# Strassen's seven products for the up projections of a streaming encoder layer

## The chip, the cores and the metric

One NeuronCore of one Trainium2 chip runs the whole layer in one launch. The metric is the device time of that launch in microseconds. Engine names below: PE is TensorE (matmul), PEld its weight loads, DVE is VectorE, ACT is ScalarE, POOL is GpSimd, SP is the engine that issues all DMAs here.

## The reference

One layer over 2048 new frames and 32 frames of a running stream (2080 tokens, model width 1024, hidden width 2816). The mixer (stick-breaking attention beside a state-space model) comes first, then the part that this change is about:

```python
def conv_ffn(h, conv_prev, p):
    gu = h @ p['w_up']                                   # (tokens, 1024) x (1024, 2 * 2816)
    gate, up = gu[..., :D_FF], gu[..., D_FF:]
    gate_c, conv_new = causal_dwconv(gate, conv_prev, p['ffn_conv_w'], p['ffn_conv_b'])   # width 3
    act = jax.nn.gelu(gate_c, approximate=True) * up
    return act @ p['w_down'], conv_new

x = x + rmsnorm(m, p['g_mix_post'])                      # m: output of the mixer
f, ffn_conv_new = conv_ffn(rmsnorm(x, p['g_ffn_pre']), ffn_conv_prev, p)
x = x + rmsnorm(f, p['g_ffn_post'])
```

All of it is float32.

## The kernel before

**Precision.** A float32 product is made of three matmuls in the fast format fp32r: each operand is split into a rounded part (hi) and the rest (lo), and `dense` issues hi x hi, hi x lo and lo x hi for each chunk of 128 of the contracted width. A weight is split once: `weight` loads the raw tile, ACT rounds it (L110), POOL subtracts (L111), and the pair is also stored to a scratch tensor in DRAM (`wS_...`). Whoever asks for the same weight later recalls hi and lo with one DMA (L106), twice the raw bytes. Three weight buffers of 128 x 2 x 8 x 128 rotate in the pool `weights`, and two raw ones.

**Blocks.** Tokens lie along the free dimension and are cut into four blocks, `SBS`: three of 512 and the last of 544, which holds the 32 frames of the running stream and is worked on as two tiles of 272 (`tiles_of`). A first phase makes the input projection and the state-space part of all blocks. Then the attention of block s+1 (`Attention.heads`) runs with the tail of block s (`Tail.stream`) as filler: a generator that yields after a few matmuls, from which `heads` takes a given number of steps per attention slot (`count` gives the sum of steps). `pin` and `mark` keep PE's filler matmuls behind the attention matmul that they follow in the program; attention is not held behind filler in that way. The tail of block 3 has no attention beside it (`alone`).

**A tail.** `stream` takes, in this order: 8 steps of what the block before still owes; the output projection of half the tokens (`out_units`, 256 wide, or 272 in block 3), then of the other half, with the residual of the first half (`residual`: normalize, add x, store to DRAM, square and sum) taken a step at a time in between; `root` and `residual` of the second half; `split`, which makes hi and lo of the unnormalized tokens times the gain (L981, L982); and the rest of what is owed, namely the down projections of the last two groups of the block before. The root of the mean square (`root`, `rstd_narrow`) isn't needed by `split`: it multiplies gate when that leaves PSUM (L1015), and up's factor cancels only in the norm after the down projection, which is told so by `rcol`. Then come the 22 hidden tiles j in groups of three (the last groups of two, or one of four in block 3). `up` makes gate j (bank `o`, 24 matmuls per token tile), the convolution over the tokens, the GeLU, up j (bank `u`), the product, and its hi and lo. After the first j of a group stands the `down` projection of the group before. `finish` normalizes and writes the block before, a step here and there.

The order of instructions on each engine is made at build time from a simulated timeline with priorities by program order. PE, DVE, ACT and POOL then work off their own lists in order, and SP issues DMAs in order, so a DMA that waits for its buffer holds up those behind it.

Of the kernel before, what the change touches and what calls it, by code (L numbers as in the profile page):

```python
# [18 lines left out]
STORE = True  # L19
WBUFS = 3  # L20
RBUFS = 2
# [39 lines left out]
class Kernel:  # L61
# [35 lines left out]
    def weight(self, pool, src, n=KC, key=None, tag=None):  # L97

        nc = self.nc
        w = pool.tile([P, 2, KC, P], F32R, name=tag or "w", bufs=1 if tag else self.wbufs)  # L100
        hi, lo = w[:, 0], w[:, 1]
        keys = key if isinstance(key, list) else [key]
        if keys[0] in self.kept:
            m = n // len(keys)
            for i, k in enumerate(keys):
                nc.sync.dma_start(w[:, :, m * i : m * i + m, :].bitcast(F32), self.kept[k][:])  # L106
            return hi, lo
        raw = self.wp.tile([P, KC, P], F32, name="wraw", bufs=RBUFS)
        nc.sync.dma_start(raw[:, :n, :], src)
        nc.scalar.copy(hi[:, :n, :], raw[:, :n, :])  # L110
        nc.gpsimd.tensor_tensor(lo[:, :n, :], raw[:, :n, :], hi[:, :n, :].bitcast(F32), op=ALU.subtract)  # L111
        if key is not None and STORE:
            d = self.kept[key] = self.dp.tile([P, 2, n, P], F32, name="wS_" + "_".join(map(str, key)))
            nc.sync.dma_start(d[:], w[:, :, :n, :].bitcast(F32))
        return hi, lo
# [4 lines left out]
    def dense(self, ps, w, x, c0, c1, ks=KC, k0=0, first=True, last=True, pin=False):  # L120
        nc = self.nc
        (whi, wlo), (xhi, xlo) = w, x
        at = lambda t, k: t[k] if isinstance(t, list) else t[:, k, :]
        for k in range(ks):
            for i, (l, r) in enumerate(((whi, xhi), (whi, xlo), (wlo, xhi))):
                mm = nc.tensor.matmul(  # L126
                    ps[:, : c1 - c0],
                    l[:, k, :],
                    at(r, k0 + k)[:, c0:c1],
                    start=first and i == 0 and k == 0,  # L130
                    stop=last and i == 2 and k == ks - 1,
                )
# [434 lines left out]
def gate(kn, s, xs, xc, r0, tm):  # L567
# [3 lines left out]
    for c in range(4):  # L571
        w = kn.weight(kn.wp, kn.a["wz"][c])
        for c0, c1 in tiles:
            n = c1 - c0
            ps = kn.po.tile([P, 512], F32, name="o")
            for k in range(KC):
                kn.dense(ps, [t[:, k : k + 1, :] for t in w], xs, c0, c1, ks=1, k0=k, first=k == 0, last=k == KC - 1, pin=s == NSB - 1)
                if len(tiles) == 1 or k % 2:
                    yield
# [317 lines left out]
class Tail:  # L897
# [7 lines left out]
    def __init__(self, kn, att, ctx, pu):  # L905
# [13 lines left out]
        self.owed = None  # L919

    def out_units(self, s, cat, half):
# [3 lines left out]
        if c0 == 0:  # L925
            self.m = [self.mp.tile([P, 544], F32, name=f"m{c}") for c in range(KC)]
            self.msq = att.tmp.tile([P, 544], F32, name="msq")
            self.w = {}
        back = list(range(KC - WBUFS, KC))
        for i, c in enumerate(range(KC) if c0 == 0 else back + list(range(KC - WBUFS))):  # L930
# [8 lines left out]
            for k in (4, 5, 6, 7, 0, 1, 2, 3):  # L939
                kn.dense(ps, [t[:, k : k + 1, :] for t in w], cat, c0, c1, ks=1, k0=k, first=k == 4, last=k == 3, pin=self.pin)  # L940
# [54 lines left out]

    def up(self, s, j, acts):
# [5 lines left out]
        wg = kn.weight(kn.wp, kn.a["wup"][j], key=("up", j))  # L1002
# [4 lines left out]
        for c0, c1 in tiles_of(nt):  # L1007
            ps = self.po[0].tile([P, 512], F32, name=self.po[1])
            for k in range(KC):
                kn.dense(ps, [t[:, k : k + 1, :] for t in wg], self.x, c0, c1, ks=1, k0=k, first=k == 0, last=k == KC - 1, pin=self.pin)  # L1010
# [26 lines left out]
        wu = kn.weight(kn.wp, kn.a["wup"][NJ + j], key=("up", NJ + j))  # L1037
        for c0, c1 in tiles_of(nt):
            ps = self.pu[0].tile([P, 512], F32, name=self.pu[1])
            for k in range(KC):  # L1040
                kn.dense(ps, [t_[:, k : k + 1, :] for t_ in wu], self.x, c0, c1, ks=1, k0=k, first=k == 0, last=k == KC - 1, pin=self.pin)
# [13 lines left out]
    def down(self, s, g, acts, tiles, end=False):  # L1055
# [10 lines left out]
        for c in range(0, KC, 2):  # L1066
            hi, lo = kn.weight(
                kn.wp, kn.a["wdn"][c // 2][:, 2 * j0 : 2 * j0 + 2 * n, :], 2 * n, key=[("dn", 6, c), ("dn", 7, c)] if n == 4 else ("dn", g, c)
            )
            for e in range(2):  # L1070
                w = hi[:, e : 2 * n : 2, :], lo[:, e : 2 * n : 2, :]
                for c0, c1 in tiles:
                    ps = self.po[0].tile([P, 512], F32, name=self.po[1])
                    for k in range(n):
                        kn.dense(ps, [t[:, k : k + 1, :] for t in w], acts, c0, c1, ks=1, k0=k, first=k == 0, last=k == n - 1, pin=self.pin)
                        if k < n - 1:
                            yield
                    dst = f[c + e][:, c0:c1]
                    if g == 0:
                        nc.scalar.copy(dst, ps[:, : c1 - c0])  # L1080
                    else:
                        nc.vector.tensor_tensor(dst, ps[:, : c1 - c0], dst, op=ALU.add)  # L1082
                    if end and s == NSB - 1 and c + e == KC - 1:
                        self.fsq1 = att.tmp.tile([P, 272], F32, name="sqt", bufs=2)
                        nc.scalar.activation(self.fsq1[:, : c1 - c0], f[KC - 1][:, c0:c1], AF.Square)
                    elif end:
# [237 lines left out]
```

## Time and profile before

| what | value |
|---|---|
| median of 3 runs | 2943.15 us (2933.8 to 2943.42) |
| span of the profiled execution | 2945.7 us, mean granted clock 0.978 |
| PE busy | 2816.0 us, 96% of the span |
| PEld, DVE, ACT, POOL busy | 82%, 58%, 42%, 43% |
| moved by DMA | 586.36 MB, 199 GB/s over the span |

The execution's own time is its span, from the first to the last instruction of the program; nothing around it is recorded here, and it stands 2.5 us above the median. By the order of time, up projections begin about 885 us (block 0), 1391 us (block 1), 1957 us (block 2) and 2512 us (block 3) after the start. In the lists below, a group's line reads: line of the kernel, engine, operation, output<-inputs, shapes, count, then busy us, mean ns of one, idle us before it and who ended it. A line of a window reads: busy us (instructions) of PE, PEld, DVE, ACT, POOL, the granted clock, the mean busy share of the DMA engines, GB/s. A line of the transfers reads: output<-input, queue, count, KB each, median us from issue to landing.

### The profile page before, as it was taken

How to read it: one execution, taken by the hardware profiler on the slowest of the kernel's cores; microseconds unless marked ns; L12 is line 12 of the kernel's file. 1: busy time of each engine (PE TensorE's matmuls, PEld its weight loads, DVE VectorE, ACT ScalarE, POOL GpSimd, SP SyncE). 2: the span in 40 equal slices, each digit the busy share in tenths (PEclk: the TensorE clock that was granted, in tenths of full speed). 3: DMA queues.
4: the chain of work that ended last, by engine and by line, in shares of the span. 5: the costliest groups of instructions: out<-in, count | busy, mean ns of one | idle time of the engine just before them, and what ended most of it. 6: DMA issues, size and time to landing. Idle time of an engine off the chain costs nothing.

```text
span 2945.7 us, 44837 instructions
## 1 busy us (share of the span) xinstructions
PE 2816.0 (96%) x16699; PEld 2427.4 (82%) x16699; DVE 1696.8 (58%) x2628; ACT 1250.6 (42%) x2534; POOL 1273.1 (43%) x1083
## 2 busy tenths in 40 slices
PE   8999999989889999999999999999999999999997
PEld 6777787977778888888788888978888889899997
DVE  7667576557774555537644455786666652623333
ACT  4344444337665444436433334664444443311111
POOL 4565555435676656547422222553223234511113
PEclk9999999989999999999999999999999999999998
DMA  5646463648677777777555556656554445755555
GB/s 179 183 143 187 145 173 120 173 131 271 223 266 246 267 266 251 271 261 249 194 190 182 179 171 212 247 175 219 179 175 165 167 160 200 242 183 172 170 183 194
DMA packets 251308, 586.36 MB, mean 199 GB/s; under 512 B 66154, under 2 KB 107762, under 8 KB 222546
## 3 DMA queue, kind: packets, MB, share of 16 engines
q1 hardware_dynamic: 251090, 583.49, 59.9%
q8 instruction: 133, 2.18, 0.3%
q14 instruction: 85, 0.70, 0.1%
HBM read 445.70 MB, written 137.69 MB: 198 GB/s over the span
## 4 chain that ended last, share of the span: by engine, by line
PE 74%; DVE 12%; DMA 7%; ACT 2%; issue 2%; POOL 1%; SPq 1%; DVEq 0%; POOLq 0%; ACTq 0%
PE o L126 36%; PE u L126 12%; PE t L126 11%; PE z L821 4%; PE pa L862 4%; PE pt L840 3%; PE o L370 2%; DVE xc L346 2%; DMA acB<-acD 1%; DVE prow L672 1%; DMA w<-wS_out 1%; DVE acB L446 1%; DVE xc L342 1%; DVE x L268 1%; DMA xr<-hS 1%
## 5 line engine op out<-in xcount | busy, mean ns | idle before, releaser
L126 PE MATMUL o<-xhi,w 128*128 128x512 f32 (+2 forms) x3968 | 1047.4, 346 | 30.1 <-ACT xhi L292 7.7
L126 PEld LDWEIGHTS o<-xhi,w 128*128 128x128 f32 x3968 | 698.2, 192 | 124.2 <-ACT xhi L292 7.7
L126 PE MATMUL o<-xlo,w 128*128 128x512 f32 (+2 forms) x1984 | 683.8, 345 | 6.9 <-DVE xlo L278 4.2
L111 POOL TENSOR_TENSOR w<-wraw,w 128x1024 fp32r<-128x1024 f32 (+2 forms) x156 | 369.0, 2366 | 228.2 <-ACT w L110 207.1
L677 POOL TENSOR_TENSOR beta<-beta,prow 128x512 f32<-128x512 f32 (+3 forms) x256 | 255.0, 998 | 429.1 <-DVE prow L672 345.5
L126 PEld LDWEIGHTS o<-xlo,w 128*128 128x128 f32 x1984 | 380.5, 192 | 51.7 <-DVE xlo L278 6.1
L1036 POOL TENSOR_TENSOR y<-y,gb 128x512 f32<-128x512 f32 (+1 forms) x88 | 115.8, 1317 | 544.4 <-ACT gb L1035 544.4
L126 PE MATMUL u<-xhi,w 128*128 128x512 f32 x1056 | 349.4, 398 | 0.0
L126 PE MATMUL o<-ah,w 128*128 128x512 f32 x992 | 342.5, 403 | 3.1 <-DVE f L1082 3.0
L845 DVE TENSOR_TENSOR wt<-pt,wt 128x512 fp32r<-128x512 f32 (+2 forms) x320 | 191.7, 602 | 156.5 <-ACT wt L844 153.9
L672 DVE TENSOR_TENSOR_SCAN prow<-gam,prow,z 128x513 f32<-128x513 f32 x192 | 245.3, 1277 | 61.5 <-ACT beta L670 58.9
L844 ACT CAST wt<-pt 128x512 fp32r<-128x512 f32 (+2 forms) x320 | 167.5, 526 | 208.7 <-PE pt L840 207.1
L126 PEld LDWEIGHTS u<-xhi,w 128*128 128x128 f32 x1056 | 199.1, 189 | 46.6
L126 PEld LDWEIGHTS o<-ah,w 128*128 128x128 f32 x992 | 187.5, 189 | 45.4 <-DVE f L1082 3.9
L669 ACT ACTIVATE gam<-z 128x512 f32<-128x512 f32 (+2 forms) x320 | 173.3, 542 | 95.5 <-PE z L821 69.8
L126 PE MATMUL u<-xlo,w 128*128 128x512 f32 x528 | 209.4, 397 | 0.0
L110 ACT CAST w<-wraw 128x1024 fp32r<-128x1024 f32 (+2 forms) x156 | 155.2, 995 | 124.7 <-PE o L126 91.3
L1028 DVE SCALAR_TENSOR_TENSOR y<-gb,cv,y 128x512 f32<-128x512 f32 (+1 forms) x176 | 160.0, 910 | 69.2 <-ACT y L1026 66.3
L126 PE MATMUL o<-al,w 128*128 128x512 f32 x496 | 196.8, 397 | 0.0
L126 PE MATMUL t<-xhi,w 128*128 128x272 f32 x960 | 189.1, 292 | 1.7 <-DMA w<-wS_out 1.3
L840 PE MATMUL pt<-ident,beta 128*128 128x128 f32 x1088 | 183.2, 279 | 7.7 <-DVE rn_v L178 4.4
L862 PE MATMUL pa<-wt,v 128*64 128x256 f32 (+3 forms) x1152 | 176.2, 283 | 12.5 <-DVE wt L845 6.9
(269 smaller groups left out, 5086.3 us busy)
## 6 DMA issues: line engine op xcount, KB each, us to landing
w<-wS_up SPq DMA_DIRECT2D x132, 1024.0 KB, 4.8
w<-wS_dn SPq DMA_DIRECT2D x72, 768.0 KB, 4.8
wS_up<-w SPq DMA_DIRECT2D x44, 1024.0 KB, 4.8
w<-wS_out SPq DMA_DIRECT2D x39, 1024.0 KB, 6.7
wraw<-wup SPq DMA_DIRECT2D x44, 512.0 KB, 5.8
k<-kS SPq DMA_DIRECT2D x80, 256.0 KB, 4.3
v<-vS SPq DMA_DIRECT2D x80, 256.0 KB, 4.2
wS_dn<-w SPq DMA_DIRECT2D x24, 768.0 KB, 4.5
```

Source lines behind the costliest of these rows:

```text
L110: nc.scalar.copy(hi[:, :n, :], raw[:, :n, :])
L111: nc.gpsimd.tensor_tensor(lo[:, :n, :], raw[:, :n, :], hi[:, :n, :].bitcast(F32), op=ALU.subtract)
L126: mm = nc.tensor.matmul(ps[:, : c1 - c0], l[:, k, :], at(r, k0 + k)[:, c0:c1], start=first and i == 0 and k == 0, stop=last and i == 2 and ...
L669: nc.scalar.activation(g[:, c0:512], z, AF.Sigmoid, scale=-0.125)
L672: nc.vector.tensor_tensor_scan(back(pr), back(g), z[:, 0:1].to_broadcast([P, n + 1]), self.kn.ones[:, 0:1] if prev is None else prev, op0= ...
L677: eng.tensor_tensor(b[:, :n], b[:, :n], pr[:, c0 + 1 : 513], op=ALU.mult)
L821: mm = nc.tensor.matmul(z[:, :n], q[:, P * b : P * b + P], k[:, :n], start=e == 0, stop=e == 1 and kc < s)
L840: mm = nc.tensor.transpose(t[:, P * j : P * j + P], w[:, P * j : P * j + P], kn.ident[:])
L844: nc.scalar.copy(hi, t)
L845: nc.vector.tensor_tensor(lo, t, hi.bitcast(F32), op=ALU.subtract)
L862: nc.tensor.matmul(av[:m, 2 * P * p + c0 : 2 * P * p + 2 * P], v[:, j, :m], wt[:, rest, j, c0:], start=kc == s and p + j + rest == 0, stop ...
L1028: nc.vector.scalar_tensor_tensor(y[:, :W], gb[:, i : i + W], kn.col(wc + i), y[:, :W], op0=ALU.mult, op1=ALU.add)
```

## The change

**Products.** For blocks 1 to 3 (`FAST`), `pair` takes the place of `up`. It makes gate j and up j together as a 2 x 2 block product: the two outputs against two halves of the contracted width (chunks 0 to 3 and 4 to 7) against two halves of the tokens (n = 256, or 272 in block 3). A variant of Strassen's scheme needs seven products of a half weight with a half token operand where there were eight. Products 1, 2 and 4 use plain half weights, 3, 5, 6 and 7 sums and differences of them. Products 2, 3 and 7 add into the PSUM bank of 1, 5 and 6 after that has been read; ACT and DVE put the parts together into gate and up.

**Weight sums.** In block 0, which keeps `up`, the raw halves of gate and up stay in their buffers until `sums` has formed the four sums in place with four DVE operations; they are stored as raw sums. In block 1 `factor` loads a raw sum, splits it as any weight and stores hi and lo; blocks 2 and 3 recall them.

**Tokens.** `normal` normalizes the tokens ahead of the products (root, multiply, then split), forms the four token combinations on DVE and splits them. `root` and `split` are no longer called for these blocks. The combinations pass through buffers of `gb`, `y` and `ub`, and two of them end in the place of `m`.

**Weights in halves.** A weight comes as tiles of four chunks (`UNIT`), six buffers and five raw ones in place of three and two of eight. The down projection's weights are laid out by single output tile and loaded one at a time instead of two. In block 3 the pairs' weights rotate through ten buffers of the pool `wkeep`. The part of memory set aside for DMA descriptors is made smaller.

```diff
+    def normal(self, s, half):
...
+        r = kn.rstd_narrow(att.tmp, *kn.bank, [self.msq[:, c0:c1]], n, D, stay=True)
+        yield
+        for k in range(KC) if c0 == 0 else (0, 1, 2, 3, 4, 5, 6, 7):
+            nc.vector.scalar_tensor_tensor(
+                M[:, k, c0:c1], M[:, k, c0:c1], kn.col(C_GFFN + k), r[:, :n], op0=ALU.mult, op1=ALU.mult
+            )
+            if c0 == 0 or k >= 4:
+                self.part(M[:, k, c0:c1], hi[k][:, c0:c1], lo[k][:, c0:c1], nc.vector if c0 and k % 2 else None)
+            if c0 == 0:
+                yield
+        if c0 == 0:
+            return
+
+        q = slice(0, 4), slice(4, 8)
+        m11, m12 = M[:, q[0], :n], M[:, q[0], n : 2 * n]
+        m21, m22 = M[:, q[1], :n], M[:, q[1], n : 2 * n]
+        sub = lambda out, a, b: nc.vector.tensor_tensor(out, a, b, op=ALU.subtract)
+        sub(m12, m12, m11)
+        for k in range(4):
+            self.part(M[:, k, c0:c1], hi[k][:, c0:c1], lo[k][:, c0:c1])
+        raw = []
+        for pool, name, w in ((self.yp, "y", 546), (self.yp, "gb", 548), (self.rp, "ub", 544)):
+            raw.append([pool.tile([P, w], F32, name=name, bufs=2)[:, : 2 * n].rearrange("p (k t) -> p k t", k=2) for _ in range(2)])
+        for i in range(2):
+            k = slice(2 * i, 2 * i + 2)
+            sub(raw[0][i], m22[:, k, :], m12[:, k, :])
+            sub(raw[1][i], raw[0][i], m11[:, k, :])
+            sub(raw[2][i], raw[0][i], m21[:, k, :])
+        t = self.mp.tile([P, KC, 544], F32R, name="m")
+        t4 = self.rp.tile([P, 4, 544], F32R, name="t4", bufs=1)
+        put = {6: t[:, 0:4], 7: t[:, 4:8], 4: t4}
...
+                self.part(src[e], h[:, k, :], l[:, k, :], nc.vector)
...
+        self.X |= {1: side(range(4), 0), 2: side(range(4, 8), 0), 3: side(range(4, 8), n), 5: side(range(4), n)}
+
+    def sums(self, j, gate, up):
...
+        op(a11, a11, a21, ALU.subtract)
+        op(a21, a21, a22, ALU.add)
+        op(a22, a22, a11, ALU.subtract)
+        op(a12, a12, a22, ALU.subtract)
+        return {7: a11, 5: a21, 6: a22, 3: a12}
+
+    def factor(self, s, j, i):
...
+        if i in (1, 2, 4):
+            key = ("up", NJ + j if i == 4 else j, 4 * (i > 1))
+            return kn.recall(self.ring(), [key], 4, self.slot())
+        key = ("sum", j, i)
+        if key in kn.kept:
+            return kn.recall(self.ring(), [key], 4, self.slot())
+        return kn.divide(self.ring(), kn.raw(self.raws[j, i][:], 4), 4, key if s < NSB - 2 else None, self.slot())
+
+    def pair(self, s, j, acts):
...
+        for i in (1, 2, 5, 6, 3, 7, 4) if j == 0 else (1, 5, 6, 2, 3, 7, 4):
+            w = self.factor(s, j, i)
+            base = {2: 1, 3: 5, 7: 6}.get(i, i)
+            if base == i:
+                ps[i] = self.bank()
+            b = ps[base]
+            for k in (0, 2):
+                kn.dense(
+                    b, w[k : k + 2], self.X[i], 0, h, k0=k, first=base == i and k == 0, last=base != i and k == 2,
+                    pin=self.pin, loose=True,
+                )
...
+            if i == 1:
+                nc.scalar.copy(p1, b)
+            elif i == 5:
+                nc.scalar.copy(v, b)
+            elif i == 6:
+                add(t, b, p1)
+            elif i == 2:
+                nc.scalar.copy(gb[:, 2 : 2 + h], b)
+            elif i == 3:
+                e = min(nt, 512) - h
+                add(gb[:, 2 + h : 2 + h + e], b[:, :e], t[:, :e])
...
+            elif i == 7:
+                add(u, b, p1)
+                nc.gpsimd.tensor_tensor(v, v, u, op=ALU.add)
+            else:
+                add(u, u, b, ALU.subtract)
...
     def up(self, s, j, acts):
...
-        wu = kn.weight(kn.wp, kn.a["wup"][NJ + j], key=("up", NJ + j))
+        wu = halves(NJ + j)
+        if s == 0 and FAST:
+            for i, t in self.sums(j, *raw).items():
+                d = self.raws[j, i] = kn.dp.tile([P, 4, P], F32, name=f"sS_{j}_{i}")
+                nc.sync.dma_start(d[:], t[:])
...
     def stream(self, s, cat):
...
-        chain = self.residual(s, a)
+        fast = s in FAST
+        chain = chained(self.residual(s, a), self.normal(s, a) if fast else ())
         for n, _ in enumerate(self.out_units(s, cat, b)):
             yield
-            if n % 4 == 0:
+            if n % 4 == 0 or fast and n % 4 == 2:
                 next(chain, None)
-        self.root(s, a)
+        for _ in chain:
+            pass
+        if not fast:
+            self.root(s, a)
         for _ in self.residual(s, b):
             pass
-        self.split(s, a)
-        self.split(s, b)
-        self.root(s, b)
+        if fast:
+            for _ in self.normal(s, b):
+                pass
+        else:
+            self.split(s, a)
+            self.split(s, b)
+            self.root(s, b)
         yield from owed
```

More of the change, by code (lines that the diff above doesn't have):

```diff
@@ L939, in out_units @@
             for k in (4, 5, 6, 7, 0, 1, 2, 3):
[L940 removed]
+                kn.dense(ps, w[k : k + 1], cat, c0, c1, k0=k, first=k == 4, last=k == 3, pin=self.pin)
                 if k != 3:
@@ L1065, in down @@
             self.fsq = att.tmp.tile([P, 544], F32, name="fsq")
-        for c in range(0, KC, 2):
-            hi, lo = kn.weight(
-                kn.wp, kn.a["wdn"][c // 2][:, 2 * j0 : 2 * j0 + 2 * n, :], 2 * n, key=[("dn", 6, c), ("dn", 7, c)] if n == 4 else ("dn", g, c)
-            )
[L1070 to L1086, printed above, removed]
-                        self.square_f(c0, c1, c + e)
-                    yield
```

212 lines of the change are left out of this document (167 added, 45 removed).

## The prediction

> **What bounds the kernel now.** I read the page first, then the grouped lines, the chain of work, windows by stage, and the order of time at the seams between blocks.
>
> ```profile
> span 2945.7 us, 44837 instructions
> PE 2816.0 (96%) x16699; PEld 2427.4 (82%) x16699; DVE 1696.8 (58%) x2628; ACT 1250.6 (42%) x2534; POOL 1273.1 (43%) x1083
> PE 74%; DVE 12%; DMA 7%; ACT 2%; issue 2%; POOL 1%; SPq 1%; DVEq 0%; POOLq 0%; ACTq 0%
> ```
>
> PE is busy for 96% of the span and holds 74% of the chain that ended last. By stage (busy us of PE, PEld, DVE, ACT, POOL; granted clock; DMA share; GB/s):
>
> ```profile
> 950.00:1000.00 50.00, 50.00 (x243) 40.86 (x242) 24.40 (x32) 23.21 (x44) 31.32 (x20) 1.00 0.80 278
> 1345.00:1400.00 55.00, 49.73 (x292) 41.64 (x290) 46.27 (x72) 38.03 (x95) 40.32 (x49) 0.97 0.73 246
> 1500.00:1550.00 50.00, 50.00 (x248) 41.31 (x247) 25.70 (x34) 16.15 (x34) 11.24 (x10) 1.00 0.55 193
> 1900.00:1965.00 65.00, 61.17 (x376) 53.20 (x375) 55.76 (x83) 44.12 (x108) 43.49 (x54) 0.95 0.64 213
> 2428.00:2448.00 20.00, 17.31 (x89) 15.96 (x88) 5.52 (x14) 2.98 (x7) 6.81 (x9) 0.74 1.01 413
> 2700.00:2750.00 50.00, 50.00 (x401) 50.00 (x400) 17.52 (x40) 9.30 (x18) 8.17 (x6) 1.00 0.50 169
> ```
>
> Inside the feed-forward stretches (block 0 at 950, block 1 at 1500, block 3 at 2700) PE never pauses, and nothing else is near full but the DMA engines in block 0 (0.80). The seams (1345, 1900) are different: VectorE is 84 to 86% busy there and PE has gaps. So shorter PE work in the stretches is worth its full length, and longer VectorE work at the seams is dangerous.
>
> **The change, part by part.** *The products.* A matmul's own duration (346 ns in the groups) includes pipeline overlap, so its price is taken from pieces of the chain (start, length, what, how many):
>
> ```profile
> 1300.14 5.69 PE o L126 x48
> 1545.97 5.60 PE o L126 x24
> 1551.57 5.60 PE u L126 x24
> 2597.42 6.02 PE o L126 x48
> 2603.44 6.03 PE t L126 x48
> ```
>
> The first is the output projection on 256 tokens: 5.69/48 = 118.5 ns. The next two are gate and up of one hidden tile (j) in block 1, 512 wide: 5.60/24 = 233.3 ns. The last two are block 3, 272 wide: 125.6 ns. The halves cost nearly half, so weight loads stay hidden though there are more of them. Before, j costs 48 x 233.3 ns = 11.20 us in blocks 1 and 2; after, 7 products x 4 chunks x 3 matmuls = 84 of 256: 9.95 us, 1.25 us less, and 44 such j give -55.0 us. In block 3, 96 x 125.6 = 12.06 becomes 84 x 125.6 = 10.55: 1.51 x 22 = -33.2 us. Together **-88 us**. Block 0 keeps its 512-wide products.
>
> *Weights by transfers.*
>
> ```profile
> w<-wS_up SPq DMA_DIRECT2D x132, 1024.0 KB, 4.8
> wS_up<-w SPq DMA_DIRECT2D x44, 1024.0 KB, 4.8
> wraw<-wup SPq DMA_DIRECT2D x44, 512.0 KB, 5.8
> k<-kS SPq DMA_DIRECT2D x80, 256.0 KB, 4.3
> ```
>
> Before, j recalls two tiles of 1024 KB (2.10 MB). After, seven half tiles of 512 KB: 3.67 MB in blocks 2 and 3, that is 370 GB/s over 9.95 us and 348 over 10.55. The window at 2428 moved 413 GB/s with the DMA engines full, so both fit; a half tile lands in some 4.5 us (between the 4.3 and 4.8 above), while the next five of six buffers give it 5 x 1.42 = 7.1 us and block 3's ring of ten gives more. Cost 0; if only the 278/0.80 = 347 GB/s of block 0's mixed reads and stores could be had, block 2 would lose 10.58 - 9.95 = 0.6 us per j, 14 us. In block 1 four of the seven are still sums: three recalls (1.57 MB), four raw loads (1.05) and four stores (2.10) make 4.72 MB per j, 475 GB/s: more than any window shows. At 413 GB/s j takes 11.4 us, 1.5 too long; 22 j give 33 us. But the DMA engines have slack in each down projection between (share 0.55 at 1500), the buffers carry some of it over, and attention can be placed there. I take **+8**, ends 0 and 81 (at 347 GB/s: 3.65 x 22).
>
> [...]
>
> *Engines beside.*
>
> ```profile
> L111 POOL TENSOR_TENSOR w<-wraw,w 128x1024 fp32r<-128x1024 f32 (+2 forms) x156 | 369.0, 2366 | 228.2 <-ACT w L110 207.1
> L278 DVE TENSOR_TENSOR xlo<-x,xhi 128x512 fp32r<-128x512 f32 (+1 forms) x24 | 25.9, 1125 | 0.4 <-ACT xhi L277 0.4
> L1015 DVE TENSOR_TENSOR gb<-t,r 128x272 f32<-128x272 f32 (+1 forms) x44 | 18.5, 421 | 77.9 <-PE t L126 75.7 <-ACT r L206 2.2
> L1034 DVE SCALAR_TENSOR_TENSOR gb<-gb,y 128x512 f32<-128x512 f32 (+1 forms) x88 | 61.7, 702 | 91.4 <-ACT gb L1033 91.2
> L126 PE MATMUL o<-ah,w 128*128 128x512 f32 x992 | 342.5, 403 | 3.1 <-DVE f L1082 3.0
> ```
>
> Evacuation in a pair: four VectorE adds of half width (4 x 0.42) in place of two wide multiplies, some +1 us per j on an engine half idle in the stretches. Block 1 puts four splits on GpSimd, 4 x 2366/2 ns = 4.7 us per j, beside 11.24 of 50 us now: hidden; with no cover it would be 104 us. What is new is the bank: product 2 adds into product 1's bank after it was read, with 24 narrow matmuls (2.8 us) between. Now the down projection has nine wide ones (2.1 us) per bank and its whole idle time for that is 3.1 us. I take **+4** (0 to 20).
>
> *Sums in block 0.* 22 x 4 VectorE operations of 512: 0.70 to 1.13 us each by the rows above, 62 to 99 us in all, beside VectorE at 24.4 of 50: hidden. They write in the raw tiles, so four of the five raw buffers are held until a store has landed. Loop: two splits (2 x 1.2), two sums (2.0), a store and a load (about 4.5 each) = 13.4 us against 11.2 us of dense PE: 2.2 us late in two of three j, 32 us at most. The window at 950 also grows in bytes (4.72 to 5.24 MB per j with the down weights), to a share near 0.89. Attention can fill such gaps: **+8**, ends 0 and 32. The extra DMA issues wait in SP's queue behind stores that wait for the sums; that is part of this term.
>
> *Tokens normalized ahead.* Now the root is applied when gate and up leave PSUM, so the products start without it. After, products wait for it. Block 3's seam (PE, POOL, ACT, DVE in order of time):
>
> ```profile
> 2507.99 3.35 DVE L963 SCALAR_TENSOR_TENSOR m<-m,cv,u 128x272 f32<-128x272 f32 x8
> 2512.51 0.40 PE L126 MATMUL t<-xhi,w 128*128 128x272 f32 x1 [0.28 <-DVE f L1082]
> 2524.09 0.76 POOL L782 TENSOR_TENSOR msq<-msq,xr 128x272 f32<-128x272 f32 x1
> 2527.36 0.86 POOL L188 TENSOR_TENSOR rn_w<-rn_v,mhalf 128x3 f32<-128x3 f32 x1 [2.51 <-DVE rn_v L178]
> 2531.50 0.39 ACT L206 COPY r<-u 128x272 f32<-128x272 f32 x1 [9.23 <-PE u L200]
> 2565.41 0.57 PE L126 MATMUL o<-xhi,w 128*128 128x272 f32 x1 [5.53 <-DMA w<-wS_up]
> ```
>
> Up starts at 2512.5, but the second half's root is there only at 2531.5. From there `normal` needs 8 multiplies (3.35), the difference of the halves (about 1.4) and its split before product 5; six more differences of about 0.7 and a split before product 6, which also frees the `y` buffer that product 1 leaves into: about 12 us. PE would go on at some 2543, 31 us late, with one or two products (3 us) done. Two things give back: the squares on GpSimd are now emitted ahead of the down projection's and may end some 5 us earlier, and the 5.5 us wait for weights at 2565 has time to vanish. I take **+20**, ends 10 and 31. Seams of blocks 1 and 2:
>
> ```profile
> 1391.17 0.40 PE L126 MATMUL o<-xhi,w 128*128 128x512 f32 x1
> 1400.87 0.42 ACT L206 COPY r<-u 128x256 f32<-128x256 f32 x1
> 1957.09 0.39 PE L126 MATMUL o<-xhi,w 128*128 128x512 f32 x1
> 1961.70 0.37 ACT L206 COPY r<-u 128x256 f32<-128x256 f32 x1 [1.42 <-PE u L200]
> ```
>
> The root comes 10 and 5 us after the first product, and the VectorE work behind it, about 20 us in place of 11 for today's split, meets an engine that is 84 to 86% busy. The first products come 25 to 30 us late. But attention of the next block is not bound to wait for them, and PE can run it in between, as it does in the seams now. I take **+6 each, +12**, ends 0 and 25 each.
>
> *The end.* The last gate is done two products (3.0 us) before the last up instead of 48 matmuls (6.0): **+3**.
>
> Sum: -88 + 8 + 4 + 8 + 20 + 12 + 3 = -33. From the profiled 2945.7 that is 2912.7. That span is 2.5 us above the median of the three runs, 2943.15, so I forecast **2910**.
>
> **The rivals.** (1) *Everything is covered.* Attention fills the seams of blocks 1 and 2, the ring and the transfers cost nothing, and only block 3's lower end (10), the end (3) and a few waits remain: -88 + 17, so 2872. For: PE at 50.00 of 50 in every stretch. Against: block 3 has no attention left to fill with.
>
> (2) *The seams stand open.* VectorE, already 86% busy there, delays attention as well, so that it cannot fill: 31 + 25 + 25 for 32 gives +49, so 2959; half of that, 2935. For: the two windows at the seams. Against: PE loses only 5 of 55 and 4 of 65 us there now.
>
> (3) *Block 1 is bound by transfers,* and slower than before. Its dense j moves 4.72 MB; at the 347 GB/s that block 0's reads and stores extrapolate to, and with no slack carried over, 81 us for 8: 2983. It decides (0.5% slower) once the rate is under 379 GB/s with nothing carried over: 12.45 us per j, 2.5 x 22 = 55 us. For: block 0's mix of reads and stores, not the pure reads at 2428, is the nearest row. Against: over a group of three j with its down projection, 3 x 5.77 = 17.3 MB in about 54 us is 320 GB/s, below even 347. [...]
>
> (4) *The raw ring holds block 0 up:* 32 us for 8, so 2934.
>
> **How the numbers follow.** The forecast, 2885 to 2928, gets 0.45; (1) 0.17; (2) 0.20; (3) 0.12; (4) 0.06. No change (within 0.5%, 14.7 us, about what a measurement can tell here: 2928.4 to 2957.9) collects (4) and nearly all of (2), slower (3) and the tail of (2): faster 0.62, same 0.24, slower 0.14. The range 2864 to 2960 leaves out the lowest third of (1) and most of (3).
>
> **What would show it.** In the chain, pieces of 84 narrow matmuls per pair in 9.9 us (10.5 in block 3) prove the products; the DMA rate in block 1's pairs, and waits of PE on weights there, price the transfers. In block 3's seam the first product 5 stands behind the split of its operand, and the idle time before it should be 15 to 30 us. In block 0, PE idle before a weight that waits for a raw tile prices the ring. I am wrong if narrow products don't run back to back, if seams cost over 80 us, or if block 1's j takes over 12 us.

## The result and the profile after

The changed kernel is slower: 2970.64 us median (2966.83 to 2973.12, 4 runs) beside 2943.28 for the kernel before (2933.8 to 2946.25, 4 runs); the ratio is 1.0095, interval 1.0075 to 1.0116. The forecast was 2910 us with a range up to 2960. The profiled execution spans 2971.3 us, 25.6 more than the one before.

The head of the page:

```profile
span 2971.3 us, 50761 instructions
PE 2761.0 (93%) x18019; PEld 2451.1 (82%) x18019; DVE 1863.9 (63%) x2915; ACT 1380.9 (46%) x2920; POOL 1521.7 (51%) x1361
```

PE has 55 us less work than before (2816.0), and the span is longer all the same: PE now waits. First, the products themselves. A piece of the chain in block 3:

```profile
2686.97 17.32 PE t L150 x138
```

And two matmuls of a product in block 2 in order of time (ten more start in the rows left out, so the second row's comes eleven steps after the first's):

```profile
2122.87 0.28 PE L150 MATMUL o<-xhi,w 128*128 128x256 f32 x1
...
2124.16 0.28 PE L150 MATMUL o<-xhi,w 128*128 128x256 f32 x1
```

17.32/138 = 125.5 ns, and 1.29/11 = 117 ns: the prices of the prediction (125.6 and 118.5). Windows: two in block 1's stretch, one in block 2's, one in the seam before block 1's products, then block 3's seam in steps of 7 us (columns as before: PE, PEld, DVE, ACT, POOL busy, granted clock, DMA share, GB/s):

```profile
1550.00:1600.00 50.00, 48.88 (x375) 45.83 (x374) 32.61 (x46) 30.35 (x68) 29.04 (x26) 1.00 0.93 344
1850.00:1890.00 40.00, 37.75 (x289) 35.94 (x287) 17.94 (x27) 15.98 (x33) 23.05 (x19) 1.00 0.96 340
2100.00:2200.00 100.00, 99.43 (x695) 91.57 (x694) 53.32 (x79) 42.02 (x90) 29.63 (x29) 1.00 0.84 283
1400.00:1450.00 50.00, 34.54 (x184) 25.18 (x185) 45.20 (x63) 36.10 (x81) 30.39 (x35) 0.84 0.34 117
2549.00:2556.00 7.00, 0.00 (x0) 0.00 (x0) 0.00 (x0) 1.25 (x3) 6.76 (x11) 0.58 0.78 263
2556.00:2563.00 7.00, 2.61 (x12) 2.40 (x12) 2.50 (x8) 0.12 (x1) 1.50 (x2) 0.50 0.19 58
2563.00:2570.00 7.00, 4.21 (x15) 3.52 (x15) 7.00 (x11) 3.21 (x9) 6.13 (x6) 0.50 0.01 2
2570.00:2577.00 7.00, 5.85 (x25) 5.21 (x24) 7.00 (x11) 3.53 (x7) 4.24 (x5) 0.50 0.39 132
2577.00:2584.00 7.00, 5.45 (x24) 5.46 (x25) 6.08 (x12) 1.73 (x7) 2.01 (x2) 0.50 0.67 205
```

Block 2, which reads all its weights split, runs as forecast (99.43 of 100). In the two windows of block 1 the DMA engines are busy for 0.93 and 0.96 at 344 and 340 GB/s. That is not the most that reads and stores moved together. Thirty us inside the first window, with eight stores of split sums among the transfers, moved 401 GB/s:

```profile
1560.00:1590.00 30.00, 29.90 (x250) 29.16 (x249) 20.23 (x28) 17.46 (x42) 19.19 (x17) 1.00 1.03 401
```

In the seam at 1400 VectorE is busy for 45.20 of 50 us, PE for 34.54, at a clock of 0.84. Block 3's seam reads like a list of waits: 7 us without any PE work while POOL adds up the squares (6.76), then VectorE at 7.00 of 7, and the clock at one half from 2556 on.

To put a number on each stage I keep a ledger. For every matmul, the time to the next matmul's start, less the median of that step for its shape in the kernel before, is "lost"; summed by stage. The medians themselves add up to the "dense work". A **seam** lasts from the block's first output projection tile to its first gate convolution, a **block** from there to the next seam; "rest" is all else. The ledger is of one execution of each kernel: in kernels that leave seam 3 as it is, that entry runs from 30.3 to 34.1, so a few us in one entry tell nothing.

| lost us | blk 0 | seam 1 | blk 1 | seam 2 | blk 2 | seam 3 | blk 3 | rest | dense work |
|---|---|---|---|---|---|---|---|---|---|
| before | 7.1 | 9.2 | 10.8 | 7.5 | 9.5 | 1.4 | 7.3 | 149.5 | 2726.4 |
| after | 13.0 | 35.5 | 45.3 | 23.9 | 13.3 | 33.4 | 3.6 | 150.9 | 2635.1 |

Dense work fell by 91.3 us; the seams lost 74.7 more, block 1 34.5 more, all else 7.4. That makes +25.3 of the 25.6 us between the spans.

### The profile page after: what moved, and what is told of

Read it like the earlier page. It is cut to its first block, busy times and chain, and to the rows that moved or that the text cites. A ratio compares the mean times of both kernels' runs of the same rounds, so it can differ in the third digit from the quotient of the medians.

```text
span 2971.3 us, 50761 instructions
## 1 busy us (share of the span) xinstructions
PE 2761.0 (93%) x18019; PEld 2451.1 (82%) x18019; DVE 1863.9 (63%) x2915; ACT 1380.9 (46%) x2920; POOL 1521.7 (51%) x1361
## 5 line engine op out<-in xcount | busy, mean ns | idle before, releaser
L150 PE MATMUL o<-xhi,w 128*128 128x256 f32 (+2 forms) x3760 | 916.0, 328 | 37.5 <-ACT xhi L315 8.0
L150 PEld LDWEIGHTS o<-xhi,w 128*128 128x128 f32 x3760 | 648.6, 192 | 103.6 <-issue 9.1
L135 POOL TENSOR_TENSOR w<-wraw,w 128x512 fp32r<-128x512 f32 (+3 forms) x332 | 521.1, 1575 | 288.6 <-ACT w L134 258.0
L150 PE MATMUL o<-xlo,w 128*128 128x256 f32 (+2 forms) x1880 | 613.6, 326 | 6.4 <-DVE xlo L301 4.2
L134 ACT CAST w<-wraw 128x512 fp32r<-128x512 f32 (+3 forms) x332 | 226.0, 683 | 185.3 <-PE o L150 106.8
L150 PE MATMUL u<-xhi,w 128*128 128x256 f32 (+1 forms) x832 | 211.9, 332 | 7.4 <-DVE y L1256 3.3
L863 PE MATMUL pt<-ident,beta 128*128 128x128 f32 x1088 | 182.1, 282 | 10.8 <-DVE beta L700 4.5
L885 PEld LDWEIGHTS pa<-wt,v 128*64 128x64 f32 (+1 forms) x1152 | 150.3, 168 | 38.7 <-DVE wt L868 14.0
L693 ACT ACTIVATE beta<-z 128x512 f32<-128x512 f32 (+2 forms) x320 | 173.3, 542 | 0.0
L844 PE MATMUL z<-k,qa 128*128 128x512 f32 (+2 forms) x320 | 141.3, 442 | 33.5 <-DVE prow L695 29.6
L150 PE MATMUL t<-ah,w 128*128 128x272 f32 (+1 forms) x768 | 165.1, 303 | 7.2 <-ACT ah L1190 4.2
```

The costliest lines, as they stand in the source:

```text
L134: nc.scalar.copy(hi, raw[:, :m, :])
L135: nc.gpsimd.tensor_tensor(lo, raw[:, :m, :], hi.bitcast(F32), op=ALU.subtract)
L150: mm = nc.tensor.matmul(ps[:, : c1 - c0], l, r, start=first and i == 0 and k == 0, stop=last and i == 2 and k == len(w) - 1, **({"skip_gro ...
L693: nc.scalar.activation(b[:, :n], z, AF.Sigmoid, scale=0.125)
L844: mm = nc.tensor.matmul(z[:, :n], q[:, P * b : P * b + P], k[:, :n], start=e == 0, stop=e == 1 and kc < s)
L863: mm = nc.tensor.transpose(t[:, P * j : P * j + P], w[:, P * j : P * j + P], kn.ident[:])
```

## Experiments

The theories put to the test: A, the loss is latency in the seams and block 1's transfers; B, the half tiles themselves cost; C, in block 1 it is the splits on ACT and GpSimd, not the bytes; D, in the seams it is VectorE's own work, not the wait for the root. Ratios are to the kernel before, measured beside each, times are medians. The median of the kernel before lay between 2938.5 and 2943.4 us, so medians of two rows compare to some 5 us, and their ratios count where that matters. The ledger of each (columns as above):

| kernel | us | ratio, interval | blk 0 | seam 1 | blk 1 | seam 2 | blk 2 | seam 3 | blk 3 |
|---|---|---|---|---|---|---|---|---|---|
| e_none | 2929.67 | 0.9955, 0.9941 to 0.997 | -0.4 | 8.3 | 5.9 | 7.4 | 8.7 | 0.9 | 7.0 |
| e_nostore | 2980.28 | 1.0129, 1.0106 to 1.0153 | 12.6 | 35.9 | 19.4 | 27.2 | 18.7 | 34.1 | 23.0 |
| e_noroot | 2939.05 | 0.9999, 0.9981 to 1.0017 | 12.7 | 29.9 | 37.1 | 21.4 | 11.8 | 21.0 | 4.8 |
| e_fast23 | 2977.42 | 1.0117, 1.0101 to 1.0134 | 15.8 | 10.8 | 11.2 | 25.8 | 21.7 | 33.7 | 22.0 |
| e_nocomb | 2928.27 | 0.9961, 0.9948 to 0.9974 | 13.8 | 20.0 | 40.1 | 12.9 | 17.4 | 13.5 | 5.9 |
| e_seamless | 2908.7 | 0.9898, 0.9881 to 0.9915 | 14.0 | 12.9 | 44.6 | 11.7 | 13.6 | 6.1 | 8.9 |
| e_sumless | 2963.36 | 1.0087, 1.0064 to 1.011 | 2.4 | 36.7 | 45.7 | 25.1 | 13.7 | 30.3 | 4.0 |
| e_rootlate | 2969.56 | 1.0103, 1.0086 to 1.012 | 12.4 | 29.3 | 26.9 | 28.7 | 39.8 | 21.0 | 10.0 |
| e_fix | 2956.19 | 1.0064, 1.0041 to 1.0087 | 15.4 | 32.7 | 45.7 | 13.8 | 13.2 | 26.5 | 5.3 |
| e_fixroot | 2960.99 | 1.0072, 1.0052 to 1.0092 | 13.2 | 31.7 | 42.1 | 26.1 | 14.8 | 15.2 | 11.5 |
| e_split0 | 3000.31 | 1.0195, 1.0177 to 1.0213 | 70.2 | 29.3 | 13.3 | 26.1 | 12.7 | 30.4 | 2.5 |
| e_fixsplit0 | 2979.37 | 1.0126, 1.0107 to 1.0145 | 69.4 | 25.5 | 12.0 | 13.3 | 17.3 | 25.1 | 4.0 |

**Without the seven products.**

```diff
-FAST = (1, 2, 3)
+FAST = ()
```

> No block takes the seven products (FAST is empty): what is left of the change is weights in halves, the down weights one tile at a time, and the smaller descriptor memory. Theory A (the loss sits in the seams between blocks and in block 1's transfers): back at the kernel before, 2943 within 12 us. Rival B (the halves themselves cost: twice as many issues on SP's queue, smaller pieces): 2960 or more, with waits of PE on weights all over.

Measured: the half tiles and the new layout of the down projection alone gain 0.45%, and this version, which keeps the whole computation, beats both kernels. So the half tiles cost nothing on balance (theory B falls); what the products bring and cost is best read against this row: dense work -91.3, blocks and seams +130.2 lost, rest +4.2.

**Block 1 without its stores.**

```diff
-        return kn.divide(self.ring(), kn.raw(self.raws[j, i][:], 4), 4, key if s < NSB - 2 else None, self.slot())
+        return kn.divide(self.ring(), kn.raw(self.raws[j, i][:], 4), 4, None, self.slot())
```

> The split weight sums are never stored: blocks 1, 2 and 3 each load the raw sums and split them on ACT and POOL. In block 1 everything stays but the four stores of 512 KB per j (5.77 MB with the down weights become 3.67); blocks 2 and 3 get the splits and move 1.05 MB per j less each. Theory A: the time PE loses in block 1's stretch (30 us over dense matmuls between 1500 and 1890 us) falls under 10, and the whole comes to 2945 within 12. Rival C (in block 1 the splits on ACT and POOL are late, not the transfers): block 1 keeps its 30 us, blocks 2 and 3 get the same, 2985 or more.

Every block now splits its sums in line and stores none. Windows over the whole stretches of blocks 0 and 1 in the changed kernel:

```profile
880.00:1305.00 425.00, 414.27 (x1983) 338.09 (x1982) 285.63 (x358) 208.52 (x437) 281.01 (x230) 0.99 0.83 284
1460.00:1905.00 445.00, 415.84 (x2870) 377.60 (x2868) 282.76 (x398) 229.25 (x492) 260.38 (x223) 0.99 0.87 311
```

The window of block 1 in this kernel:

```profile
1464.00:1878.00 414.00, 401.77 (x2834) 371.16 (x2833) 270.30 (x384) 218.96 (x472) 254.50 (x214) 0.99 0.71 231
```

What SP's queue waited for in block 3 of this kernel (line, waited for: us, times, longest):

```profile
SPq L114 <- POOL w L135: 103.2, 56, 4.9
```

Block 1 goes from 45.3 to 19.4 us lost with the DMA share from 0.87 to 0.71: the stores cost 26. Of the 45.3, 11.7 were PE's named waits for weights (6.6 for up's, 5.1 for down's). But blocks 2 and 3 pay for splitting again (+5 and +19). SP waits 103.2 us for GpSimd's splits, with recalls behind them in its queue, yet PE's costliest named wait from 2600 to 2920 us is one of 3.8, for VectorE to empty a bank: what it waits for recalled weights is less. So what the splits delay there stays open. Neither expectation came: theories A and C both hold a part.

**Blocks 2 and 3 only.**

```diff
-FAST = (1, 2, 3)
+FAST = (2, 3)
```

> Only blocks 2 and 3 take the seven products; block 1 recalls whole weights as before the change, and blocks 2 and 3 split raw sums, which nobody stores. Theory A: block 1's account (27 us less matmul work, 57 us more lost time) goes away, 30 us: 2941 within 12. Rival C: the splits, now in blocks 2 and 3, cost there what they cost in block 1: 2965 or more.

Seam 1 and block 1 return to 10.8 and 11.2, and blocks 2 and 3 lose 21.7 and 22.0, splitting in line with no store: rival C's number. Read together: in these kernels a block that recalls loses 4 to 13 us, one that splits 19 to 23, one that splits and stores 45.

**Without the root.** It leaves the root of the norm before the up projection out of blocks 1 to 3.

```diff
-        r = kn.rstd_narrow(att.tmp, *kn.bank, [self.msq[:, c0:c1]], n, D, stay=True)
...
-            nc.vector.scalar_tensor_tensor(
-                M[:, k, c0:c1], M[:, k, c0:c1], kn.col(C_GFFN + k), r[:, :n], op0=ALU.mult, op1=ALU.mult
+            nc.vector.tensor_scalar(
+                M[:, k, c0:c1], M[:, k, c0:c1], kn.col(C_GFFN + k), 0.0, op0=ALU.mult, op1=ALU.add
```

> Leaves the root mean square before the feed-forward part out for blocks 1 to 3: the tokens are only multiplied by the gain, so their combinations don't wait for the squares' sum; the combinations and their splits stay. Theory A with the root as the seams' cause: each of the three seams gets 12 to 20 us back, 2925 within 12. Rival D (VectorE's own added work in the seams delays, not the wait for the root): under 10 us come back in all, 2962 or more.

The root is worth 32 us in the medians. The ledger, whose execution was the fastest of ten (2931.16), has 20.5 less lost in the seams, 8 less in block 1, and 6 of the root's own matmuls (dense work 2629.0). The three seams got 5.6, 2.5 and 12.4 back, between the two expectations. 72.3 us stay lost there: the root is not the larger part.

**Without the token combinations.**

```diff
-        sub(m12, m12, m11)
...
-            sub(raw[0][i], m22[:, k, :], m12[:, k, :])
-            sub(raw[1][i], raw[0][i], m11[:, k, :])
-            sub(raw[2][i], raw[0][i], m21[:, k, :])
...
+        self.X = {6: side(range(4), 0), 7: side(range(4, 8), n), 4: side(range(4, 8), 0)}
```

> Leaves out the token combinations of each normalizing step: the five differences and the splits of products 6, 7 and 4's operands; these products multiply the plain quarters instead, so the number of matmuls, the weight loads and the root's wait stay. In the changed kernel the three seams lose 92.8 us against dense matmuls (35.5, 23.9, 33.4; without the Strassen blocks 8.3, 7.4, 0.9). Theory A (the seams cost what the root's wait and the latency of the chain cost): leaving out the root saved 21 us there, so the combinations' VectorE time is mostly the rest: seams fall by 35 to 55 us, time about 2925 to 2940. Theory D2 (the combinations stand under the first products 1, 5 and 2, and what the seam lacks is the splits of the plain operands and the order of the queue): seams fall by under 15 us, time 2955 to 2970.

42 us in the medians, 46.4 in the three seams: half of what the seams lose. Theory A's number, and D2 falls. What the products wait for stands in block 3's seam of the changed kernel, in order of time (start, length, engine and line, idle time before and who ended it):

```profile
2556.69 1.15 PE L192 MATMUL u<-ones,msq 128*128 128x1 f32 x6 [10.98 <-POOL msq L805]
2558.24 0.86 POOL L211 TENSOR_TENSOR rn_v<-rn_v,mhalf 128x3 f32<-128x3 f32 x1 [1.60 <-DVE rn_v L201]
2560.71 3.36 DVE L1038 SCALAR_TENSOR_TENSOR m<-m,cv,u 128x272 f32<-128x272 f32 x8 [2.61 <-issue]
2565.78 0.59 PE L150 MATMUL o<-xhi,w 128*128 128x272 f32 x1 [0.58 <-ACT xhi L1024]
2567.10 1.34 DVE L1051 TENSOR_TENSOR y<-m 128x544 f32<-128x544 f32 x2
2572.65 4.68 DVE L1319 SCALAR_TENSOR_TENSOR f<-f,cv,rstd 128x256 f32<-128x256 f32 x8
2577.25 1.24 DVE L1025 TENSOR_TENSOR t<-ub,t 128x544 fp32r<-128x544 f32 x1
2578.55 1.73 PE L150 MATMUL t<-t,w 128*128 128x272 f32 x6 [2.66 <-DVE t L1025]
```

The root's matmul waits 10.98 us for the squares, whose adds share GpSimd with those of the previous block's down projection; then one chain on VectorE, and in it the eight multiplies of the previous block's last step (L1319, 4.68 us) stand ahead of the split that a product waits for (L1025).

**Without both.**

> Leaves out both: the root of the norm before the up projection (tokens are scaled by the gain alone) and the token combinations of the run above. If the two account for the seams, these fall from 92.8 us of lost time to about 25 (the kernel without Strassen blocks has 16.6), time about 2970 - 32 - 40 = 2900. If another thing in the seams (attention run ahead in them, the out projection's own splits, the first pair's transfers) stands behind the rest, 50 us stay there and the time is about 2925.

The edits of the last two together. 2908.7 us: the seams lose 30.7 where some 25 were expected. Seams 1 and 3 in windows:

```profile
1304.00:1415.00 111.00, 103.38 (x747) 95.71 (x746) 75.76 (x112) 68.52 (x173) 78.57 (x99) 0.97 0.77 258
2438.00:2521.00 83.00, 79.29 (x557) 74.98 (x556) 33.94 (x67) 32.85 (x90) 55.46 (x71) 0.98 0.77 258
```

The same stages of the changed kernel:

```profile
1305.00:1461.00 156.00, 135.55 (x921) 118.69 (x920) 109.08 (x164) 97.33 (x234) 103.03 (x122) 0.93 0.60 198
2478.00:2594.00 116.00, 93.60 (x607) 88.11 (x606) 54.56 (x113) 39.37 (x102) 65.57 (x81) 0.84 0.62 204
```

Combinations and root together make 62 of the 92.8 us; the kernel without the products has 16.6, so 14 us of the seams stay unattributed. Block 1 still loses 44.6: its cost is its own.

**Block 0 without the sums.** The raw quarters are stored unsummed; loads and stores stay, and no store waits for a sum.

```diff
-        op(a11, a11, a21, ALU.subtract)
-        op(a21, a21, a22, ALU.add)
-        op(a22, a22, a11, ALU.subtract)
-        op(a12, a12, a22, ALU.subtract)
```

> Leaves out the four VectorE sums of weights per hidden column in block 0 and stores the raw quarters in their place: the same tiles held, the same stores and reads. Against the kernel without Strassen blocks, block 0's stretch loses 13 us more. If VectorE's 96 sums stand in the way (they delay the evacuations of the matmul banks behind them): block 0's lost time falls to about 0 to 3 us, time 2958 to 2962. If the raw tiles held longer, or their stores, do it: no change in block 0, time 2970.

Block 0 falls from 13.0 to 2.4: the loss goes with the sums (88 of them, not the 96 of the expectation), while the bytes stay. The medians differ by 7 us and the ratios by 0.0008, within their intervals, so this rests on the ledger. How the sums cost it is not shown. In the changed kernel's block 0 PE waits 3.3 us for VectorE to empty up's bank and never for a weight from a raw tile; its longest wait, 5.4 us, is at the end, for the output projection's weights, while the DMA engines are full (share 1.00 from 1285 to 1306 us). Without the sums, PE's waits for these weights up to 1300 us are 2.0 us in all.

**The root at the evacuation, and the stores one block later.**

```diff
...
-                nc.scalar.copy(gb[:, 2 : 2 + h], b)
+                add(gb[:, 2 : 2 + h], b, self.r[:, 0:h], ALU.mult)
...
+            self.root(s, a)
+            self.root(s, b)
...
-        return kn.divide(self.ring(), kn.raw(self.raws[j, i][:], 4), 4, key if s < NSB - 2 else None, self.slot())
+        return kn.divide(self.ring(), kn.raw(self.raws[j, i][:], 4), 4, key if s == NSB - 2 else None, self.slot())
```

> Two changes that keep the whole computation: tokens of blocks 1 to 3 go unnormalized into their products, and the root is applied where the gate's halves leave the matmul banks (and at the end of the block for the rest), so that no product waits for it; and the split weight sums are stored in block 2 in place of block 1 (blocks 1 and 2 split them in line, block 3 recalls). From the runs with one of these: the root's wait gave 32 us; block 1 without its stores 26 us, of which block 2 gives back 5 for its splits, and block 2's stores cost at most what block 1's did (26) and perhaps little, since block 2's reads are as many. Sum 2970 - 25 - 26 + 5 + (0 to 26): 2925 to 2950. If block 1's loss was the stores' share of the DMA engines alone, block 2 now shows it: about 2945; if it was their collision with the rest of block 1, 2925.

No gain: more time than either expectation. Block 1 loses 18 less and block 2, which now splits and stores, 26 more: the cost moves with the stores. The seams fall by 13.8 only, and block 3 gives 6.4 of it back, where the root's multiplications now stand at each evacuation.

**The combinations off the path.** Four quarter tiles in place of one, combinations in place, columns 0 and 1 together with products 1, 2, 5 and 3 of both ahead of 6, 7 and 4; and the same with the root at the evacuation.

```diff
+        g = [self.pair(s, j, acts, True) for j in (0, 1)]
+        for _ in islice(g[0], 8):
+            yield
+        self.later(6)
+        for _ in islice(g[1], 8):
+            yield
+        self.later(7)
+        self.later(4)
```

> Keeps the computation and moves the token combinations off the path. The tokens are held as four quarter tiles; the combinations are made in the place of the quarters (one in two spare buffers), so that the first pair of columns no longer waits for its own buffers gb, y and ub, which the changed kernel used as scratch; columns 0 and 1 of each block run together, first products 1, 2, 5 and 3 of both (8 products of 1.42 us, 11.3 us, that need plain quarters or the one difference), then 6, 7 and 4 of both, and the splits for these are issued between. Leaving the combinations out gave 42 us, 46 of it in the seams. If those are a matter of order (theory A: latency and queue heads), hiding them gives 25 to 40 us: 2930 to 2945. If VectorE simply has too much to do in a seam (theory D), the work is only moved and delays the evacuations behind it: under 12 us, 2958 to 2970.

> The kernel above with tokens that go unnormalized into the products and the root applied where the gate's halves leave the matmul banks. In the run that had this and the moved stores, the seams fell from 92.8 to 79.0 us; leaving the root out took the seams from 92.8 to 72.3. So 10 to 20 us below the kernel above: 2915 to 2930 by theory A. By theory D, which has VectorE as what the seam is short of, the root's three multiplications per column add to it: no lower than the kernel above.

14 us in the medians, 9 by the ratios (1.0095 to 1.0064): under theory A's 25, and at theory D's bound of 12 within the noise. The seams lose 73.0 in place of 92.8. The gain is in seams 2 and 3; seam 1, where VectorE is 45.20 of 50 us busy, gains 2.8. With the root at the evacuation as well it is no lower (2960.99), which is what theory D said. So part of the combinations' price was order; the 27 us that the seams still lose over the kernel without combinations fit VectorE's time itself (theory D), though no run isolates that.

**The sums split where they are made,** in block 0; and that together with the kernel above.

```diff
-                d = self.raws[j, i] = kn.dp.tile([P, 4, P], F32, name=f"sS_{j}_{i}")
-                nc.sync.dma_start(d[:], t[:])
+                kn.divide(kn.wp, t, 4, ("sum", j, i))
```

> The sums of the weights are split into hi and lo and stored in block 0, where they are made, in place of the raw store; blocks 1 to 3 only read them back (92 MB fewer... in numbers: block 0 stores 45 MB in place of 22, block 1 reads 45 MB and stores none in place of reading 22 and storing 45). If block 1's loss (45.3 us against dense matmuls) was its own in-line splits and stores, block 1 becomes like block 2, whose stretch loses 13 us: a gain of 32 there. Block 0 moves 284 GB/s in its stretch at a DMA share of 0.83; 22 MB more over 425 us is 53 GB/s, 337 in all, just under the 340 to 344 that mixed reads and stores reached in block 1. Theory A (the loss is the stores' load of the DMA engines, wherever they stand): block 0 loses 15 to 30 us more, time 2955 to 2972. Theory C (it is the splits' place between reads and products, which only block 1 has): block 0 loses under 10 us more, time 2938 to 2948.

> The run above with the combinations moved as in the kernel with quarter tiles and paired first columns, which gave 14 us by itself. If both parts add: 14 us under the run above, so 2924 to 2934 by theory C and 2941 to 2958 by theory A. It beats the kernel without Strassen blocks (2929.7) only in the first case.

Both missed: block 1 falls to 13.3 as expected, the level of block 2, and block 0 loses 57 more, far beyond either theory. Block 0's and block 1's stretches, and SP's waits in block 0:

```profile
888.00:1362.00 474.00, 430.71 (x1936) 343.63 (x1935) 338.12 (x355) 254.57 (x523) 411.38 (x315) 0.94 0.82 297
1516.00:1917.00 401.00, 393.80 (x2789) 363.08 (x2788) 237.77 (x370) 173.88 (x381) 128.01 (x125) 0.99 0.81 280
```

```profile
SPq L138 <- POOL w L135: 226.0, 141, 7.6
```

The same row of SP's waits in block 1 of the changed kernel:

```profile
SPq L138 <- POOL w L135: 81.8, 47, 6.6
```

And in block 1 without its stores (`e_nostore`, 1464 to 1878 us), where SP's loads of raw sums wait for the splits:

```profile
SPq L114 <- POOL w L135: 128.4, 72, 6.0
```

The DMA share in block 0 is 0.82, no fuller than the changed kernel's 0.83. What is full is GpSimd (411.38 of 474 us). PE's longest waits in that window, and what VectorE waited for before it could empty up's bank (L1255):

```profile
PE u L150 <- DVE y L1255: 16.1, 7, 3.5
PE o L150 <- ACT w L134: 8.6, 5, 3.5
PE o L150 <- POOL w L135: 6.3, 6, 2.5
```

```profile
  POOL y L1243: 17.9, 10
```

So PE's longest waits lead to GpSimd and to the splits of weights, not to bytes. SP's 226.0 us are no evidence: the same kind of wait is there in block 0 of the kernel before (887 to 1300 us), which loses 7.1 us:

```profile
SPq L114 <- POOL w L111: 262.9, 64, 8.4
```

No run isolates GpSimd, and a rival is untested: the split sums take buffers of the same six as the up weights, and they are stored from there. In block 1, too, SP's wait for GpSimd is not the price by itself: without the stores it grew from 81.8 to 128.4 us while the block lost 26 us less. Whether the stores cost by their bytes or by what they keep waiting stays open. The two parts of the last kernel do add (seam 2 at 13.3, block 1 at 12.0), and it is slower than before all the same.

## Why the prediction was wrong

By its own steps, the profiled executions compared (before to after):

| step | forecast | measured |
|---|---|---|
| products | -88 | -91.3 dense work |
| block 1's transfers | +8 | +34.5 |
| banks and evacuation | +4 | +0.1 (blocks 2 and 3) |
| sums in block 0 | +8 | +5.9 (block 0) |
| block 3's seam | +20 | +32.0 |
| seams of blocks 1 and 2 | +12 | +42.7 |
| end and the rest | +3 | +1.4 |
| sum | -33 | +25.3 |

- **Right:** the products, the banks, block 0 in size and the end. Block 0's size is luck in part: I had the held raw tiles and the store's loop as the term and took VectorE's time for the sums as hidden, but PE never waited for a weight from a raw tile, and the loss went with the sums. The half tiles, which I priced at nothing, gained 13 us by themselves (0.45%), so the products' own cost in block 0 is 13, not 6.
- **The step that failed first** is "attention of the next block is not bound to wait for them, and PE can run it in between". Attention was there (35 of the score matmuls `z<-k,qa` fell into seam 1, 16 before), but its own steps wait for VectorE too: PE sat idle ahead of its score matmuls for VectorE's scan 6.2 us in 11 waits, against 1.3 in 3 before (last part of this section); with its other named waits for VectorE that is 13.3 of the 35.5 us lost, against 4.6 of 9.2. The term was +12 and measured +42.7. The prediction had quoted the engine as 84 to 86% busy in those windows and still counted 9 us more work on it as covered; leaving the combinations out gave 46 us in the seams.
- **Second,** "the buffers carry some of it over" in block 1: the term was +8 and measured +34.5. Of that, 26 go with the stores, whether by their bytes or by what waits on them. The rest fits splitting in line, which I had as "hidden": a block that splits without storing loses 19 to 23 us, one that recalls 4 to 13. Rival (3) named the block, but its rate is not a ceiling: the whole stretch moved 311 GB/s at a share of 0.87, and 30 us with stores in them 401. That 413 GB/s with nothing carried over would give 33 us, nearly what came, is no proof of that sum.
- **Block 3's seam** had its mechanism right, at the bound (32.0, upper end 31): product 5's first matmul (2565.78) waits for its split, 20 us after product 1's end (2545.71), with only matmuls of norms between. The squares did not end 5 us earlier: counted from the first tile of the output projection (2448.2 before, 2478.1 after), the root's first result on GpSimd came 79.2 us in before (2527.36) and 80.1 after (2558.24). Three of the six differences that I took at 0.7 us measured 1.28 to 1.30 (last section). And a term was missing, the clock (below); its price is not isolated.
- **The chances.** Rival (2) priced the open seams at 31 + 25 + 25 = 81; 74.7 came. I held it and rival (3) for alternatives, at 0.20 and 0.12. They came together, each in good part, since nothing in the one excludes the other: with the measured 74.7 for 32 and 34.5 for 8, the same sum gives +36, and a span of 2982.

The rows of the score matmuls' idle time in seam 1 (until what: us, times), of the changed kernel and of the kernel before:

```profile
  DVE prow L695: 6.2, 11
```

```profile
  DVE prow L672: 1.3, 3
```

## What to carry to other kernels

Fewer matmuls paid here only where PE was the limit (91.3 us less dense work, 74.7 us more lost in the seams), so price the preparation in the stage where it must be done: here VectorE, at 84 to 86% busy, had no cover to give, and the attention that was to fill PE's gap used the same engine. Two rivals that don't exclude each other should be added, not weighed against each other. A long wait of the DMA queue need not be a loss: SP waited 262.9 us for GpSimd in block 0 of the kernel before, which lost 7.1. Read what PE waits for.

## What the hardware showed that I had not expected

- **PE's half clock outlasted its gap.** After the 10.98 us gap in block 3's seam the granted clock stays at 0.50 from the window at 2556 through the one at 2577, although PE is busy 5.85 of 7 us in one of them. The window at 2549, at 0.58, puts the fall to half some 1.1 us after that window's start, 4.4 us after PE's last matmul (2545.71). PE worked without a wait from 2570.35 to 2575.88 (5.5 us), with four one-column matmuls of a norm among the others, and stayed at half; it worked without a wait again from 2578.55, and full clock came back at 2584.2, 5.7 us later. What brings it back is not shown. At half clock matmuls of 272 columns started 227 ns apart, at full clock 125.
- **Reads and stores mixed had no one rate.** With the DMA engines full, 30 us of block 1 moved 401 GB/s (share 1.03) and ten others (1750 to 1760 us) 332 at a share of 0.99; 20 us of pure reads in the kernel before (from 2428 us) moved 413 at 1.01.
- **VectorE's sums of two SBUF operands took longer beside GpSimd,** 1.21 us in the median against 0.67 to 0.69. In the kernel with sums split in block 0, the sums' 80 operations in the window took 1.37 us on average, while those of the same width that empty up's bank, with one operand in PSUM, took 0.67 to 0.69, though GpSimd was busy for 411.38 of that window's 474 us:

```profile
L1081 DVE TENSOR_TENSOR wraw<-wraw 128x512 f32<-128x512 f32 x80 | 109.8, 1372 | 14.7 <-POOL w L135 13.4
L1255 DVE TENSOR_TENSOR y<-u,y x22: 673/680/692, 896.4 to 1347.5; 128x512 f32<-128x512 f32 x22
```

In the changed kernel's block 0, 23 of the 88 sums ran with GpSimd idle and took 0.67 to 0.69 us; 24 ran with GpSimd at work throughout, with a median of 1.21, though five of these took 0.68 to 0.69. The prediction's price for a sum, 0.70 to 1.13, did not ask what GpSimd does meanwhile.
- **A stage that PE fills came to wait for GpSimd:** with the sums split in block 0, GpSimd was busy for 411 of 474 us and block 0 lost 57 us more. PE's longest waits there, 16.1 us for VectorE, lead to it by VectorE's 17.9 us of waits for GpSimd.
